# A one-layer streaming encoder: where cross attention's operands, some sums, the first weight and the last stores stand

## The chip, the cores and the metric

The kernel runs on one core of a Trainium2 chip. The metric is the time of one execution on the device in microseconds; the time before is a median of three runs. The engines are named as in the profile: PE multiplies matrices and PEld loads its stationary operand, DVE, ACT and POOL work on vectors, SP issues most of the transfers between DRAM and the core's memory. An engine runs its instructions in the order in which they stand in its row; between engines, semaphores make one wait for another.

## The reference

One layer is applied to 1024 prompt frames and 32 sample frames, which share the weights. Cut to what matters:

```python
h = rms_norm(x, g_mix)
q, k, v, ch, cb, cc, ga, gb = split(h @ w_in)
a = window_attention(q, k, v) @ w_attn_out
bo = (cb * causal_conv3(cc * ch)) @ w_conv_out
x = x + (sigmoid(ga) * a + sigmoid(gb) * bo) @ w_mix_out
cq = rms_norm(x, g_cross) @ w_cq              # 4 heads of 64
p = softmax(cq @ mem_k.T * 64 ** -0.5)        # 256 memory tokens
x = x + (p @ mem_v) @ w_co
x = x + relu(rms_norm(x, g_mlp) @ w_up) ** 2 @ w_down
y = rms_norm(x, g_final)
```

The width is 1024 and the hidden width of the MLP 4096, all in FP32. The memory's keys and values are computed from the prompt's memory tokens, and given as a cache for the sample.

## The kernel before

**Products.** An FP32 operand is split in a rounded high part and the rest, and a product is made of three matmuls: high by high, high by low and low by high (`gemm`, lines 195 to 197, and `product`, 866 to 868). The 1056 frames are treated as three chunks, `CH`, of 384, 384 and 288 columns, with the features on the partitions. A feature block of an output takes eight groups of three matmuls.

**Weights.** A block of 128 output features is a tile of 128 x 1024, 512 KB. `fetch_w` (L155) lets SP load it to `wr`; `issue_w` has ACT cast the high part `wh` (L129) and DVE subtract the low part `wl` (L130). Two raw tiles take turns, with a third at times, and two weights are made ready ahead (`LOOK`). For weights that come again with the next chunk, the dict `kept` holds low parts: at the first use `wl` is stored to DRAM (L174), later it is loaded (L168) and only the cast is done (L169).

**Start.** `norm_x` loads the first chunk's x (`raw`, L302) in four pieces, the parameters `prm` (L304) and the first weights, all on SP. ACT and DVE make the high and low parts of each feature of x (`X`, L274 and L275): two features, then the first weight, then six.

**Middle.** Per chunk, `trunk` gives eight products conv_out (`do_conv_out`: evacuation L1051, addition L1052, split to `M`) and eight products mix (`do_mix`: L1066, with x loaded by L1062). Cross attention takes its keys from `mem_key` (loads L1077) and its values from `mem_val` (load L1086, cast L1089, subtraction L1090); `mem_load` and `mem_load_s` do all of one kind at a place of the program. Scores are L1141, exponents L1146, output products L1204 to L1206 with the evacuation L1208. The first products of the MLP run beside the third chunk's trunk and cross attention: their evacuations are L1325 to L1356. `sums_early(k)` makes sums of normalised x for a later step of the MLP (L1380 to L1383, split by L1374 and L1375), `late_tiles` and `sums_first` the sums of the last columns.

**End.** `final_last` scales six tiles of 128 x 512 by the last norm (L1829 on DVE, L1831 on ACT), and SP stores them (L1833).

**Order.** The program is written as items: products are fillers, and between them come the calls that `then(i, ...)` and the third argument of `beside` put behind filler i. A scheduler that simulates the engines moves instructions among each other where data allow it; what stands in `pin` keeps the order of the program, and in a `manual_schedule` region the named engines keep the order written. So a call's place is a wish for most instructions and binding for pinned ones.

Of the kernel before, what the change touches and what calls it, by code (L numbers as in the profile page):

```python
# [10 lines left out]
F32 = mybir.dt.float32  # L11
# [7 lines left out]
P = 128  # L19
# [4 lines left out]
NF = 8  # L24
# [16 lines left out]
def hybrid_step(ctx: ExitStack, tc: tile.TileContext, io):  # L41
    nc = tc.nc
    act, dve, pool_e, pe, sp = nc.scalar, nc.vector, nc.gpsimd, nc.tensor, nc.sync
# [3 lines left out]
    def nm(s):  # L47
        uid[0] += 1
        return f"{s}_{uid[0]}"
# [12 lines left out]
    wp = ctx.enter_context(tc.tile_pool(name="wp", bufs=3))  # L62
# [31 lines left out]
    mk_d = dram.tile([2, P, 256], F32, name="mk_d")  # L94
    mv_d = dram.tile([2, P, 256], F32, name="mv_d")

    def pin(ins):
        return tc.keep_in_program_order(ins)
# [29 lines left out]
    def split(hi, lo, src):  # L128
        act.copy(hi, src)  # L129
        dve.tensor_sub(lo, src, hi.bitcast(F32))  # L130
# [26 lines left out]
            pin(load)  # L157
        fetched.append(raw)

    def issue_w():  # L160
        if not fetched:
            fetch_w()
        raw = fetched.pop(0)
        key = worder[wpos[0]]
        hi = wp.tile([P, 1024], F32R, tag="wh", name=nm("wh"))
        lo = wp.tile([P, 1024], F32R, tag="wl", name=nm("wl"))
        if kept.get(key) is not None:
            sp.dma_start(lo.bitcast(F32), kept[key])  # L168
            act.copy(hi, raw)  # L169
        else:  # L170
            split(hi, lo, raw)
            if key in kept:
                kept[key] = dram.tile([P, 1024], F32, name=nm("wl_d"))
                sp.dma_start(kept[key], lo.bitcast(F32))  # L174
        ready.append((worder[wpos[0]], (hi, lo)))
        wpos[0] += 1
# [101 lines left out]
    W = {}  # L278
# [11 lines left out]
    def norm_x():  # L290
        pool_e.memset(ones, 1.0)
        act.copy(ones_r, ones.to_broadcast([P, P]))
        warm = misc.tile([P, 1], F32, name="warm")
        act.activation(warm, ones, AF.Sqrt)
        make_identity(nc, ident)
        raws = []

        def load_x():
            for c, (o, n) in enumerate(CH):
                raw = raw_tile()[:, : NF * n].rearrange("p (f t) -> p f t", f=NF)  # L300
                for h in range(4):
                    sp.dma_start(raw[:, 2 * h : 2 * h + 2], io[f"x{c}"][:, 2 * h : 2 * h + 2])  # L302
                    if c == h == 0:
                        sp.dma_start(prm, io["params"])  # L304
                        fetch_w()
                if c == 0:
                    fetch_w()
                    fetch_w()
                raws.append(raw)

        def parts(c, fs, pinned=lambda x: x):
            for f in fs:
                xg[c][f] = (slot(xpool, f"X{c}", CH[c][1]), slot(xpool, f"X{c}", CH[c][1]))
                scaled_split(*xg[c][f], raws[c][:, f], G_MIX + f, pinned)

        def squares(c):
            n = CH[c][1]
            acc = st.tile([P, n], F32, tag="sum", bufs=2, name=nm("sum"))
            for f in range(NF):
                sq = st.tile([P, n], F32, tag="sq", bufs=2, name=nm("sq")) if f else acc  # L320
                (pin if c else lambda x: x)(act.activation(sq, raws[c][:, f], AF.Square))
                if f:
                    dve.tensor_add(acc, acc, sq)
            accs[c] = [acc]

        with tc.manual_schedule(engines={mybir.EngineType.SP}):
            load_x()
        with tc.manual_schedule(engines={mybir.EngineType.Activation, mybir.EngineType.DVE}):
            parts(0, range(2))
            issue_w()  # L330
            parts(0, range(2, NF))
            issue_w()
            issue_w()
            squares(0)
        wk, wv = ready[0][1], (ready[1][1], ready[2][1])
        kt = at_tile([P, NT], F32, "kt")
        ktt[0] = kt
        vs3 = {}

        def scaled(c):  # L340
# [731 lines left out]

    def mem_key(src, tag, bufs=1):

        t = cr.tile([P, 256], F32, tag="mkr", bufs=1, name=nm("mkr"))
        for e in range(2):
            sp.dma_start(t[64 * e : 64 * e + 64], src)  # L1077
        hi = cr.tile([P, 256], F32R, tag=f"{tag}h", bufs=bufs, name=nm("mkh"))
        lo = cr.tile([P, 256], F32R, tag=f"{tag}l", bufs=bufs, name=nm("mkl"))
        split(hi, lo, t)  # L1080
        return hi, lo

    def mem_val(src, tag):

        t = cr.tile([P, 256], F32, tag="mkr", bufs=1, name=nm("mvr"))
        sp.dma_start(t, src)  # L1086
        v = cr.tile([P, 4, 2, 64], F32R, tag=tag, name=nm("mv"))
        s3 = t.rearrange("p (h d) -> p h d", h=4)
        act.copy(v[:, :, 0], s3)  # L1089
        dve.tensor_sub(v[:, :, 1], s3, v[:, :, 0].bitcast(F32))  # L1090
        return v

    pkeys, pvals, svals = [], [], []

    def mem_load():
        pkeys.extend(mem_key(mk_d[h // 2, 64 * (h % 2) : 64 * (h % 2) + 64], "pk", 4) for h in range(4))
        pvals.extend(mem_val(mv_d[j], f"pv{j}") for j in range(2))

    def mem_load_s():
        svals.extend(mem_val(io["cmem_v"][j], f"sv{j}") for j in range(2))  # L1100

    qc, co = {}, [[None, None] for _ in CH]

# [509 lines left out]

    def cross_steps(c):

        steps = [("call", [mem_load if c == 0 else mem_load_s])]
        steps.append(("call", [lambda: chunk_stats(c)]))
        steps.append(("items", [(do_cq(c, j), ("w_cq", j)) for j in range(2)]))
        for i, step in enumerate(cross_units(c)):
            steps.append(step)  # L1620
            if i < 4 - c:
                steps.append(("call", []))
        if c:
            steps.append(("call", []))
# [23 lines left out]
        ]  # L1648

    for name, n in (("w_conv_out", NF), ("w_mix", NF), ("w_cq", 2), ("w_co", 2)):  # L1650
        kept.update(((name, j), None) for j in range(1, n, 2) if (name, j) != ("w_conv_out", 5))

    trunks = [trunk(c) for c in range(3)]
    trunks[0].insert(NF, trunks[1].pop(0))
    left = beside(
        [], trunks[0], [(i, lambda: pump(2)) for i in range(NF)] + [(12, lambda: third.update(n=0, pool=W["pool"]))]
    )
    item(lambda: pump(0))
    left = beside(cross_steps(0), trunks[1])
# [14 lines left out]
    def then(i, *what):  # L1674
        at.setdefault(i, []).extend(what)

    call = lambda fn, *args: lambda: item(lambda: fn(*args))
    assert len(left) == 1
    then(0, *[call(x) for x in left[0][1]], call(mem_load_s))
    then(1, call(chunk_stats, 1))  # L1680
    then(2, *[lambda j=j: item(do_cq(1, j), ("w_cq", j)) for j in range(2)])
    for f in range(NF):
# [19 lines left out]
    then(34, lambda: item(do_co(2, 0), ("w_co", 0)))  # L1702
    then(35, lambda: item(do_co(2, 1), ("w_co", 1)))
    for k in range(4):
        then(34 + k, call(sums_early, k))
    then(36, call(open_late), call(chunk_col, 2))
    then(37, call(chunk_row, 2))
    then(38, call(late_tiles))
# [96 lines left out]
    def final_last(c):  # L1805
# [19 lines left out]
        for i, (j, h) in enumerate([(0, 1), (1, 1), (2, 1), (0, 0), (1, 0), (2, 0)]):  # L1825
            tag, bufs = homes[i]
            y = wp.tile([P, 512], F32, tag=tag, bufs=bufs, name=nm("y"))
            if i % 2:
                dve.tensor_scalar_mul(y, turned[j][:, h], RC[c][:, j : j + 1])  # L1829
            else:  # L1830
                act.mul(y, turned[j][:, h], RC[c][:, j : j + 1])  # L1831
            rows = slice(96, P) if j == 2 else slice(0, P)
            sp.dma_start(io[f"y{c}"][j, rows, 512 * h : 512 * h + 512], y[rows])  # L1833

    A11, A21, A12, A22 = (0, 0), (0, 4), (1, 0), (1, 4)
    steps = [(j, t) for j in range(4) for t in range(2)]
# [151 lines left out]
```

## Time and profile before

| what | value |
|---|---|
| median of 3 runs (lowest to highest) | 1761.08 us (1759.91 to 1767.39) |
| the profiled execution | 1762.53 us, span 1760.8 |
| granted PE clock, mean | 0.996 |
| DMA over the span | mean 198 GB/s, 348.18 MB |

Times in rows are microseconds from the span's start. A row of the timeline gives the start, the duration, engine, line, operation, the output and inputs by the program's names, and in brackets how long the engine stood idle before it and what it waited for. Rows marked x2 or x6 are several alike. The rows of the stretches give for each engine busy time and, in brackets, the number of instructions; then the granted clock, the share of the DMA engines and the rate. SP's rows are the requests, not the transfers themselves.

### The profile page before, as it was taken

Reading aid. Unit: us, or ns where it says so; the run is one execution under the profiler, and the core shown is the slowest. Engines: PE = TensorE matmul, PEld = TensorE weight load, DVE = VectorE, ACT = ScalarE, POOL = GpSimd, SP = SyncE. Lnnn points to the kernel's source line nnn. Section 1 sums busy time; section 2 is a strip of 40 time slices with the busy share of each in tenths; the row PEclk is TensorE's granted clock in tenths of the full one; section 3 lists DMA queues with packets and bytes.
Section 4 is the critical chain, followed back from the end, with each engine's and each line's share of the span. In section 5 each row is a group of like instructions: output and inputs, shape, how many; then the busy total and the mean of one; then the engine's idle time right before and its main releaser. Section 6 shows DMA issues by size and latency. Waiting matters only on the chain.

```text
span 1760.8 us, 32586 instructions
## 1 busy us (share of the span) xinstructions
PE 1726.3 (98%) x12250; PEld 1710.8 (97%) x12250; DVE 1189.4 (68%) x2272; ACT 853.7 (48%) x1660; POOL 585.0 (33%) x667
## 2 busy tenths in 40 slices
PE   8999999999999999999899999999999999999998
PEld 8999999999999999999899999999999999999998
DVE  6776776768666647546567777787666686546675
ACT  8653534535335325335456665774444464333443
POOL 0026366453552545441225132005555410000121
PEclk9999999999999999999999999999999999999999
DMA  5243334333436888867755667675666786554554
GB/s 184 95 131 124 118 132 152 118 135 127 157 142 206 292 288 298 265 218 251 265 200 198 233 215 237 217 245 195 221 221 222 229 313 201 183 195 161 198 169 159
DMA packets 179997, 348.18 MB, mean 198 GB/s; under 512 B 18672, under 2 KB 100880, under 8 KB 179712
## 3 DMA queue, kind: packets, MB, share of 16 engines
q1 hardware_dynamic: 164272, 292.42, 49.6%
q0 software_dynamic: 15568, 53.68, 8.6%
q8 instruction: 96, 1.57, 0.4%
q14 instruction: 61, 0.50, 0.1%
HBM read 251.77 MB, written 93.67 MB: 196 GB/s over the span
## 4 chain that ended last, share of the span: by engine, by line
PE 52%; DMA 4%; DVE 2%; ACT 2%; POOL 1%; issue 1%; DVEq 0%; SPq 0%; POOLq 0%; ACTq 0%
PE acc L1773 6%; PE acc L1774 6%; PE acc L1775 6%; PE acc L866 5%; PE acc L867 5%; PE acc L868 5%; PE acc L195 3%; PE acc L197 2%; PE acc L196 2%; PE pc L867 2%; PE pc L868 2%; PE pc L866 2%; DMA ct<-m_d 1%; DMA ct<-in_x 1%; PE pa L196 1%
## 5 line engine op out<-in xcount | busy, mean ns | idle before, releaser
L129 ACT CAST wh<-wr 128x1024 fp32r<-128x1024 f32 x228 | 239.4, 1050 | 419.6 <-PE acc L1774 128.6
L130 DVE TENSOR_TENSOR wl<-wr,wh 128x1024 fp32r<-128x1024 f32 x228 | 295.6, 1296 | 130.9 <-ACT wh L129 129.3
L195 PE MATMUL acc<-X,wh 128*128 128x384 f32 (+1 forms) x864 | 282.1, 326 | 8.0 <-ACT wh L129 8.0
L196 PE MATMUL acc<-X,wh 128*128 128x384 f32 (+1 forms) x864 | 279.2, 323 | 0.0
L197 PE MATMUL acc<-X,wl 128*128 128x384 f32 (+1 forms) x864 | 278.6, 322 | 0.2 <-DVE wl L130 0.2
L271 POOL TENSOR_TENSOR xacc<-xacc,ct 128x384 f32<-128x384 f32 (+1 forms) x56 | 75.5, 1351 | 382.2 <-ACT ct L269 380.6
L195 PEld LDWEIGHTS acc<-X,wh 128*128 128x128 f32 x864 | 163.1, 189 | 8.6 <-ACT wh L129 8.0
L196 PEld LDWEIGHTS acc<-X,wh 128*128 128x128 f32 x864 | 163.4, 189 | 0.6
L197 PEld LDWEIGHTS acc<-X,wl 128*128 128x128 f32 x864 | 163.0, 189 | 0.8 <-DVE wl L130 0.8
L195 PE MATMUL acc<-Y,wh 128*128 128x384 f32 (+1 forms) x432 | 140.4, 327 | 4.1 <-DVE ct L1051 3.3
L197 PE MATMUL acc<-Y,wl 128*128 128x384 f32 (+1 forms) x432 | 140.5, 326 | 2.4 <-DMA wl<-wl_d 2.4
L196 PE MATMUL acc<-Y,wh 128*128 128x384 f32 (+1 forms) x432 | 140.5, 326 | 0.0
L1774 PE MATMUL acc<-n,wh 128*128 128x264 f32 x352 | 100.2, 285 | 0.0
L1773 PE MATMUL acc<-n,wh 128*128 128x264 f32 x352 | 100.2, 285 | 0.0
L1775 PE MATMUL acc<-n,wl 128*128 128x264 f32 x352 | 99.9, 284 | 0.0
L129 ACT CAST PTh<-pt 128x512 fp32r<-128x512 f32 (+3 forms) x94 | 45.8, 517 | 110.8 <-PE pt L584 109.7
L721 POOL TENSOR_TENSOR ws<-ws 128x256 f32<-128x256 f32 x100 | 93.1, 931 | 5.8 <-DMA ws<-in_w_up 0.2
L721 POOL TENSOR_TENSOR xacc<-xacc 128x256 f32<-128x256 f32 x100 | 87.6, 876 | 5.7 <-DMA xacc<-in_w_in 0.3
L195 PEld LDWEIGHTS acc<-Y,wh 128*128 128x128 f32 x432 | 82.0, 190 | 5.3 <-DVE ct L1051 4.2
L197 PEld LDWEIGHTS acc<-Y,wl 128*128 128x128 f32 x432 | 82.3, 191 | 2.8 <-DMA wl<-wl_d 2.8
L196 PEld LDWEIGHTS acc<-Y,wh 128*128 128x128 f32 x432 | 82.1, 190 | 0.3 <-DVE Y L777 0.3
L570 ACT ACTIVATE S<-S,nmx 128x257 f32<-128x257 f32 (+1 forms) x132 | 64.2, 488 | 20.7 <-DVE nmx L565 19.4
(424 smaller groups left out, 5503.1 us busy)
## 6 DMA issues: line engine op xcount, KB each, us to landing
wr<-in_w_in SPq DMA_DIRECT2D x53, 512.0 KB, 3.6
wr<-in_w_up SPq DMA_DIRECT2D x53, 512.0 KB, 4.7
wr<-wsum_d SPq DMA_DIRECT2D x40, 512.0 KB, 3.4
wr<-in_w_conv_out SPq DMA_DIRECT2D x24, 512.0 KB, 4.5
wr<-in_w_mix SPq DMA_DIRECT2D x24, 512.0 KB, 5.0
wr<-in_w_down SPq DMA_DIRECT2D x24, 512.0 KB, 3.5
n_d<-Z SPq DMA_DIRECT2D x32, 264.0 KB, 4.4
xacc<-in_w_down POOLq DMA_DIRECT2D x16, 512.0 KB, 4.2
```

The source lines that it names most:

```text
L129: act.copy(hi, src)
L130: dve.tensor_sub(lo, src, hi.bitcast(F32))
L195: pe.matmul(out, wh[:, a], hi, start=(k == 0), stop=False)
L196: pe.matmul(out, wh[:, a], lo, start=False, stop=False)
L197: pe.matmul(out, wl[:, a], hi, start=False, stop=(k == len(acts) - 1))
L721: pin(pool_e.tensor_tensor(t[:, to], t[:, x], t[:, y], op=ALU.add))
L866: pe.matmul(acc, wh[:, a], hi, start=(start and k == 0), stop=False, skip_group_check=True)
L867: pe.matmul(acc, wh[:, a], lo, start=False, stop=False, skip_group_check=True)
L868: pe.matmul(acc, wl[:, a], hi, start=False, stop=(k == 3), skip_group_check=True)
L1773: pe.matmul(a, wh[:, s], hi, start=(t == 0 and k == 0), stop=False, skip_group_check=True)
L1774: pe.matmul(a, wh[:, s], lo, start=False, stop=False, skip_group_check=True)
L1775: pe.matmul(a, wl[:, s], hi, start=False, stop=(t == 1 and k == 7), skip_group_check=True)
```

## The change

1. **First weight.** Its request stands in ACT's row, ahead of everything there, and no more in SP's. One feature of x is split before it in place of two, and the weight is split in two pieces, 256 and 768 columns.
2. **Operands of cross attention.** Four keys and two values of the memory and two values of the sample are loaded one per mix product of the first chunk. Their splits are pinned, and their raw tiles have two buffers in place of one.
3. **Kept low parts.** The conv_out weight 3 is no more among them: each chunk splits it again.
4. **Early sums.** `sums_early(k)` stands behind filler 35 + k in place of 34 + k.
5. **Last stores.** Those of tiles that ACT scales are requested by ACT.

The core of the diff:

```diff
-    def issue_w():
+    def issue_w(pieces=(slice(0, 1024),)):
...
-            split(hi, lo, raw)
+            for at in pieces:
+                split(hi[:, at], lo[:, at], raw[:, at])
...
                         sp.dma_start(prm, io["params"])
-                        fetch_w()
...
+        first_raw = wp.tile([P, 1024], F32, tag="wr", bufs=2, name=nm("wr"))
+        with tc.manual_schedule(engines={mybir.EngineType.Activation}):
+            act.dma_start(first_raw, weight(worder[0]))
+        fetched.append(first_raw)
...
-            parts(0, range(2))
-            issue_w()
-            parts(0, range(2, NF))
+            parts(0, range(1))
+            issue_w((slice(0, 256), slice(256, 1024)))
+            parts(0, range(1, NF))
...
-        t = cr.tile([P, 256], F32, tag="mkr", bufs=1, name=nm("mkr"))
+        t = cr.tile([P, 256], F32, tag="mkr", bufs=2, name=nm("mkr"))
...
-        split(hi, lo, t)
+        if bufs == 4:
+            pin(act.copy(hi, t))
+            pin(dve.tensor_sub(lo, t, hi.bitcast(F32)))
+        else:
+            split(hi, lo, t)
...
-        act.copy(v[:, :, 0], s3)
-        dve.tensor_sub(v[:, :, 1], s3, v[:, :, 0].bitcast(F32))
+        pin(act.copy(v[:, :, 0], s3))
+        pin(dve.tensor_sub(v[:, :, 1], s3, v[:, :, 0].bitcast(F32)))
...
-        steps = [("call", [mem_load if c == 0 else mem_load_s])]
+        steps = [("call", [])]
...
-        [], trunks[0], [(i, lambda: pump(2)) for i in range(NF)] + [(12, lambda: third.update(n=0, pool=W["pool"]))]
+        [], trunks[0], [(i, lambda: pump(2)) for i in range(NF)]
+        + [(12, lambda: third.update(n=0, pool=W["pool"]))] + [(NF + 1 + i, fn) for i, fn in enumerate(mem_loads)]
...
-    then(0, *[call(x) for x in left[0][1]], call(mem_load_s))
+    then(0, *[call(x) for x in left[0][1]])
...
-        then(34 + k, call(sums_early, k))
+        then(35 + k, call(sums_early, k))
...
-            sp.dma_start(io[f"y{c}"][j, rows, 512 * h : 512 * h + 512], y[rows])
+            (sp if i % 2 else act).dma_start(io[f"y{c}"][j, rows, 512 * h : 512 * h + 512], y[rows])
```

Beside these, `mem_loads` is a list of the eight loads, each a call of `mem_key` or `mem_val`, and `("w_conv_out", 3)` joins the exception in the loop that fills `kept`. The lines of the changed kernel are shifted: L1051, L1066, L1086, L1090, L1208, L1380 and L1833 become L1055, L1070, L1094, L1098, L1215, L1387 and L1841.

ACT's row at the start, before, where `wr` is the loaded first weight and `X` the parts of x:

```order
L292 ACT_TABLE_LOAD
L292 CAST ones_r<-ones 128x128
L294 ACT_TABLE_LOAD
L294 ACTIVATE warm<-ones 128x1
L274 ACTIVATE X_7_165<-raw_140,prm 128x384
L274 ACTIVATE X_9_169<-raw_140,prm 128x384
L129 CAST wh_173<-wr_143 128x1024
L274 ACTIVATE X_13_177<-raw_140,prm 128x384
```

and now:

```order
L328 DMA wr_138<-in_w_in 128x1024
L293 ACT_TABLE_LOAD
L293 CAST ones_r<-ones 128x128
L295 ACT_TABLE_LOAD
L295 ACTIVATE warm<-ones 128x1
L275 ACTIVATE X_7_168<-raw_145,prm 128x384
L129 CAST wh_172<-wr_138 128x256
L129 CAST wh_172<-wr_138 128x768
L275 ACTIVATE X_11_178<-raw_145,prm 128x384
```

The request leads the row, and one `X` stands ahead of the weight's two casts.

DVE's row at the last conv_out products of the first chunk and the first mix products, before. The first number of a name is the buffer or copy; `mv` are values, `wl` weights, `M` and `Y` activations:

```order
L797 TENSOR_TENSOR Y_1654_9618<-ct_9569,Y_1653_9617 128x288
L1090 TENSOR_TENSOR mv_10177<-mvr_10175,mv_10177 128x4x64
L130 TENSOR_TENSOR wl_9728<-wr_9725,wh_9727 128x1024
L130 TENSOR_TENSOR M_9662<-ct_9658,M_9661 128x384
L797 TENSOR_TENSOR Y_1666_9666<-ct_9621,Y_1665_9665 128x288
L797 TENSOR_TENSOR Y_1668_9670<-ct_9623,Y_1667_9669 128x288
L1090 TENSOR_TENSOR mv_10182<-mvr_10180,mv_10182 128x4x64
L1051 TENSOR_TENSOR ct_9710<-acc_9685,Gb_1562_9252 128x384
L1051 TENSOR_TENSOR ct_9760<-acc_9735,Ga_1110_6654 128x384
L1052 TENSOR_TENSOR ct_9710<-ct_9710,ct_9683 128x384
L130 TENSOR_TENSOR wl_9770<-wr_9767,wh_9769 128x1024
L130 TENSOR_TENSOR M_9714<-ct_9710,M_9713 128x384
```

and now from the addition of the first chunk's eighth conv_out product (L1052 before, L1056 now) on; `mkl` are keys:

```order
L1056 TENSOR_TENSOR ct_9713<-ct_9713,ct_9686 128x384
L130 TENSOR_TENSOR wl_9731<-wr_9728,wh_9730 128x1024
L130 TENSOR_TENSOR M_9717<-ct_9713,M_9716 128x384
L801 TENSOR_TENSOR Y_1679_9721<-ct_9676,Y_1678_9720 128x288
L801 TENSOR_TENSOR Y_1681_9725<-ct_9678,Y_1680_9724 128x288
L1055 TENSOR_TENSOR ct_9763<-acc_9738,Ga_1110_6659 128x384
L130 TENSOR_TENSOR wl_9773<-wr_9770,wh_9772 128x1024
L130 TENSOR_TENSOR M_9767<-ct_9763,M_9766 128x384
L1070 TENSOR_TENSOR Ga_1696_9803<-acc_9778,ct_9776 128x384
L130 TENSOR_TENSOR wl_9820<-wr_9817,wh_9819 128x1024
L276 SCALAR_TENSOR_TENSOR Y_1698_9806<-Ga_1696_9803,prm,Y_1697_9805 128x384
L1086 TENSOR_TENSOR mkl_9814<-mkr_9810,mkh_9813 128x256
```

The value that stood ahead of L1051 is gone from there; the first key follows the first mix product's evacuation (L1070) and low part.

DVE's row at the end of the third chunk's cross attention, before, where `Ga` and `Gb` are the evacuated output products and `ct` the sums:

```order
L1208 TENSOR_TENSOR Ga_2186_11851<-acc_13550,Ga_2186_11851 128x288
L1208 TENSOR_TENSOR Ga_2216_11977<-acc_13561,Ga_2216_11977 128x288
L1208 TENSOR_TENSOR Gb_2233_12045<-acc_13572,Gb_2233_12045 128x288
L1380 TENSOR_TENSOR ct_13583<-n_2546_13460,n_2554_13468 128x240
L1208 TENSOR_TENSOR Gb_2252_12138<-acc_13634,Gb_2252_12138 128x288
L1381 TENSOR_TENSOR ct_13584<-t_2538_13452,ct_13583 128x240
L1382 TENSOR_TENSOR ct_13585<-t_2538_13452,n_2546_13460 128x240
L130 TENSOR_TENSOR wl_13631<-wr_13628,wh_13630 128x1024
L1208 TENSOR_TENSOR Gb_2271_12228<-acc_13645,Gb_2271_12228 128x288
L1383 TENSOR_TENSOR ct_13586<-n_2562_13476,ct_13584 128x240
L1208 TENSOR_TENSOR Gb_2304_12380<-acc_13655,Gb_2304_12380 128x288
```

and now:

```order
L1215 TENSOR_TENSOR Ga_2215_11980<-acc_13564,Ga_2215_11980 128x288
L1215 TENSOR_TENSOR Gb_2232_12048<-acc_13575,Gb_2232_12048 128x288
L1215 TENSOR_TENSOR Gb_2251_12141<-acc_13621,Gb_2251_12141 128x288
L130 TENSOR_TENSOR wl_13618<-wr_13615,wh_13617 128x1024
L1215 TENSOR_TENSOR Gb_2270_12231<-acc_13632,Gb_2270_12231 128x288
L1215 TENSOR_TENSOR Gb_2303_12383<-acc_13642,Gb_2303_12383 128x288
L1215 TENSOR_TENSOR Gb_2316_12438<-acc_13652,Gb_2316_12438 128x288
L1387 TENSOR_TENSOR ct_13662<-n_2545_13463,n_2553_13471 128x240
L1388 TENSOR_TENSOR ct_13663<-t_2537_13455,ct_13662 128x240
L1389 TENSOR_TENSOR ct_13664<-t_2537_13455,n_2545_13463 128x240
L130 TENSOR_TENSOR wl_13681<-wr_13678,wh_13680 128x1024
```

Three of the evacuations stood behind the first sums; now all stand ahead of them.

More of the change, by code (lines that the diff above doesn't have):

```diff
@@ L1079, in mem_key @@
         lo = cr.tile([P, 256], F32R, tag=f"{tag}l", bufs=bufs, name=nm("mkl"))
-        split(hi, lo, t)
+        if bufs == 4:
[3 more added lines that the diff above has]
+            split(hi, lo, t)
         return hi, lo
     def mem_val(src, tag):
-        t = cr.tile([P, 256], F32, tag="mkr", bufs=1, name=nm("mvr"))
+        t = cr.tile([P, 256], F32, tag="mkr", bufs=2, name=nm("mvr"))
         sp.dma_start(t, src)
@@ L1088, in mem_val @@
         s3 = t.rearrange("p (h d) -> p h d", h=4)
-        act.copy(v[:, :, 0], s3)
-        dve.tensor_sub(v[:, :, 1], s3, v[:, :, 0].bitcast(F32))
+        pin(act.copy(v[:, :, 0], s3))
+        pin(dve.tensor_sub(v[:, :, 1], s3, v[:, :, 0].bitcast(F32)))
         return v
     pkeys, pvals, svals = [], [], []
[L1095 to L1100, printed above, removed]
+    mem_loads = [
+        lambda h=h: pkeys.append(mem_key(mk_d[h // 2, 64 * (h % 2) : 64 * (h % 2) + 64], "pk", 4)) for h in range(4)
+    ]
+    mem_loads += [lambda j=j: pvals.append(mem_val(mv_d[j], f"pv{j}")) for j in range(2)]
+    mem_loads += [lambda j=j: svals.append(mem_val(io["cmem_v"][j], f"sv{j}")) for j in range(2)]
     qc, co = {}, [[None, None] for _ in CH]
@@ L1650, in hybrid_step @@
     for name, n in (("w_conv_out", NF), ("w_mix", NF), ("w_cq", 2), ("w_co", 2)):
-        kept.update(((name, j), None) for j in range(1, n, 2) if (name, j) != ("w_conv_out", 5))
+        kept.update(((name, j), None) for j in range(1, n, 2) if (name, j) not in (("w_conv_out", 3), ("w_conv_out", 5)))
     trunks = [trunk(c) for c in range(3)]
```

## The prediction

> **What bounds the kernel now.** I read the page's busy times first, then PE's waits, then the timeline around each of them. PE's row says that the kernel is PE time with small holes.
>
> ```profile
> PE 1726.3 (98%) x12250; PEld 1710.8 (97%) x12250; DVE 1189.4 (68%) x2272; ACT 853.7 (48%) x1660; POOL 585.0 (33%) x667
> PE acc L195 <- ACT wh L129: 8.0, 1, 8.0
> PE acc L195 <- DVE ct L1051: 5.0, 4, 1.9
> PE acc L866 <- ACT lt L1355: 2.8, 2, 1.7
> PE sc L1141 <- ACT S L1146: 1.1, 1, 1.1
> ```
>
> PE is idle 1760.8 − 1726.3 = 34.5 us of the span: 8.0 before the first matmul, about 7.5 after the last (tail rows below), and some 19 in holes of at most 2.5. The change adds and removes no matmul of the products, so it can gain only from these 34.5 us. The columns of the last four rows are: us in total, times, longest; two more waits, of 2.45 and 1.90, stand below with their places.
>
> **The start.** Four rows set the end of the first hole; the others show what follows.
>
> ```profile
> 0.74 0.40 SPq L302 DMA_DIRECT2D raw<-in_x  x1
> 1.20 0.41 SPq L304 DMA_DIRECT2D prm<-in_params  x1
> 1.66 0.42 SPq L155 DMA_DIRECT2D wr<-in_w_in  x1
> 4.34 1.12 ACT L274 ACTIVATE X<-raw,prm 128x384 fp32r<-128x384 f32 x2 [0.52 <-DMA prm<-in_params]
> 6.92 1.04 ACT L129 CAST wh<-wr 128x1024 fp32r<-128x1024 f32 x1 [1.45 <-DMA wr<-in_w_in]
> 7.99 1.22 DVE L130 TENSOR_TENSOR wl<-wr,wh 128x1024 fp32r<-128x1024 f32 x1 [1.86 <-ACT wh L129]
> 8.01 0.69 PE L195 MATMUL acc<-X,wh 128*128 128x384 f32 x1 [8.01 <-ACT wh L129]
> 9.13 3.26 DVE L275 SCALAR_TENSOR_TENSOR X<-raw,prm,X 128x384 fp32r<-128x384 f32 x6
> 10.72 0.52 PE L195 MATMUL acc<-X,wh 128*128 128x384 f32 x1
> 11.04 0.52 PE L196 MATMUL acc<-X,wh 128*128 128x384 f32 x1
> 13.32 0.34 PE L195 MATMUL acc<-X,wh 128*128 128x384 f32 x1
> 13.50 0.33 PE L196 MATMUL acc<-X,wh 128*128 128x384 f32 x1
> ```
>
> The weight, asked for at 1.66, is what ACT waits for (1.45 us), and PE waits for the cast. The change moves that request to ACT's first row, at about 0.73 (SP's first is at 0.74), 0.93 earlier. If all of it reaches the landing, the weight is there at 5.99. The casts' price comes from two lengths: 1024 columns take 1.04 and 384 take 1.12/2 = 0.56, so about 0.27 + 0.75 per 1000 columns: 0.46 for the piece of 256 and 0.85 for 768. DVE's two pieces are about 0.45 and 0.96 by the same way (1.22; 3.26/6 = 0.54). The first matmul starts at 5.99 + 0.46 = 6.45. But the second feature's high part now stands behind both casts and its low part behind both subtractions: casts to 7.30, X high to 7.86, subtractions to 8.33, X low to 8.87. PE waits there, ends the second feature's group of three matmuls at 0.32 each by 9.5, and starts the third at 9.5; before it was 10.72. That is 1.2 early.
>
> The other end: raw, prm and the weight now share the transfer engines. If the weight lands only when before all three had, at 6.92, only the pieces are gained: the third group starts at 10.47, 0.25 early. PE's pace changes within these rows, from 0.32 (10.72 to 11.04) to 0.18 (13.32 to 13.50). If the change of pace stays at its hour, work moved ahead of it is worth half: 0.13 to 0.6; if it comes earlier with the start, up to 2.0. A loss is possible if prm is held back too: landed with the others at 6.92, it lets X of feature 0 end at 7.5, the first cast at 7.9, the second at 8.8, the second feature's X at 9.4 and its low part, behind both subtractions, at about 10.4; the third group then starts at 11.0, 0.3 late. SP's own later requests come 0.42 earlier, without the weight's row among them, which nothing here waits for. I take −0.7, the middle of early and late landing with most of the pace; the ends are −2.0 and +0.3.
>
> [...]
>
> **Cross attention's operands.** Eight loads and their splits were scattered; four of the values stand here.
>
> ```profile
> 837.05 0.32 SPq L1086 DMA_DIRECT2D mvr<-mv_d  x1
> 840.78 0.41 ACT L1089 CAST mv<-mvr 128x256 fp32r<-128x256 f32 x1 [2.83 <-DMA mvr<-mv_d]
> 841.22 0.43 DVE L1090 TENSOR_TENSOR mv<-mvr,mv 128x256 fp32r<-128x256 f32 x1 [1.86 <-ACT mv L1089]
> 842.17 0.45 PE L195 MATMUL acc<-M,wh 128*128 128x384 f32 x1 [1.64 <-DVE ct L1051]
> 849.46 0.41 ACT L1089 CAST mv<-mvr 128x256 fp32r<-128x256 f32 x1 [2.66 <-DMA mvr<-in_cmem_v]
> 850.35 1.14 SPq L1077 DMA_DIRECT2D mkr<-in_cmem_k  x2
> 852.13 0.44 PE L197 MATMUL acc<-M,wl 128*128 128x384 f32 x1 [0.50 <-DVE wl L130]
> 866.83 1.23 DVE L130 TENSOR_TENSOR wl<-wr,wh 128x1024 fp32r<-128x1024 f32 x1
> 868.98 0.89 SPq L168 DMA_DIRECT2D wl<-wl_d  x1
> 876.12 0.44 PE L197 MATMUL acc<-Y,wl 128*128 128x384 f32 x1 [2.45 <-DMA wl<-wl_d]
> 842.00:878.00 36.00, 32.71 (x180) 31.75 (x181) 21.59 (x32) 16.98 (x30) 7.57 (x6) 0.98 0.75 259
> ```
>
> At 837.05 SP asks for a value; ACT stands 2.83 us for it and DVE 1.86, and the evacuation L1051 behind them lets PE wait 1.64. The same at 849.46 delays a weight: 0.50. The order now has nothing of memory ahead of the last conv_out evacuations, so I take both as gone: 2.14. The new splits, 0.41 on ACT and 0.43 on DVE in each of eight mix products, fit: DVE works 21.59 of 36 us there, and eight splits add 3.4 to that at most.
>
> The 2.45 is the end of a late stream: the low part, asked for at 868.98 behind its weight's split of 866.83, lands at 876.1, 7.1 later. With PE 2.14 ahead, it must land by 871.5. SP's rows of operands, such as the 1.14 at 850.35 ahead of the next weight, are now asked for by the place of their split, and I let the stream come one mix product earlier: 24 matmuls at 0.17 to 0.18, or 4.2 us. A landing at 871.9 leaves 0.4. So 2.0 of 2.45 gained, and −4.1 together. The ends: 0, if the operands wait as before, and −4.6 (2.14 + 2.45).
>
> **One kept low part less.** It takes away a store and two reloads of 512 KB and adds two subtractions of 1.22. In the third chunk it falls into this stretch:
>
> ```profile
> 975.40:979.70 4.30, 4.30 (x30) 4.30 (x30) 0.16 (x2) 1.49 (x3) 0.00 (x0) 1.00 1.02 374
> ```
>
> DVE works 0.16 of 4.30 us while PE is never idle: the subtraction costs nothing, and 1.2 if that cover is gone. I leave it at 0.
>
> **Sums one place later.** Before, the first of them stand between the evacuations of the last cross output product.
>
> ```profile
> 1138.50 0.98 DVE L1380 TENSOR_TENSOR ct<-n,n 128x240 f32<-128x240 f32 x1
> 1139.78 0.39 DVE L1381 TENSOR_TENSOR ct<-t,ct 128x240 f32<-128x240 f32 x1
> 1140.09 1.01 DVE L1382 TENSOR_TENSOR ct<-t,n 128x240 f32<-128x240 f32 x1
> 1141.02 1.82 DVE L130 TENSOR_TENSOR wl<-wr,wh 128x1024 fp32r<-128x1024 f32 x1
> 1142.77 0.44 DVE L1208 TENSOR_TENSOR Gb<-acc,Gb 128x288 f32<-128x288 f32 x1
> 1143.26 0.39 PE L866 MATMUL acc<-Y,wh 128*128 128x264 f32 x1 [1.90 <-DVE Gb L1208]
> 1150.40 0.41 DVE L1383 TENSOR_TENSOR ct<-n,ct 128x240 f32<-128x240 f32 x1 [2.42 <-PE pq L226]
> 1161.68 1.23 DVE L130 TENSOR_TENSOR wl<-wr,wh 128x1024 fp32r<-128x1024 f32 x1 [1.08 <-ACT wh L129]
> ```
>
> All eight L1208 now stand ahead of the first sum, so the 1.90 goes. About 2.4 us of DVE's work (0.98 + 0.39 + 1.01) moves behind them; the 2.42 and 1.08 of idle time later take it. The last key of the sample, fetched earlier now, puts its scores ahead, and I count half of the 1.1 us at L1141. The 2.8 at L1355 is ACT's crowd of copies and stays. Sum −2.5. The ends: −4.7 (1.9 + 1.1 + 1.7), if the longer L1355 wait and the rest of L1141's go too, and +3, if the fourth group of sums meets the late ones.
>
> **The tail.**
>
> ```profile
> 1754.21 1.84 ACT L1831 ACTIVATE y<-acc,rc 128x512 f32<-128x512 f32 x3 [0.89 <-DVE rc L233]
> 1754.23 2.12 DVE L1829 TENSOR_SCALAR y<-acc,rc 128x512 f32<-128x512 f32 x3
> 1754.93 2.77 SPq L1833 DMA_DIRECT2D out_y<-y  x6
> ```
>
> Six requests take 2.77 on SP, 0.46 each, to 1757.70; the span ends 3.1 later. With three on ACT, in its row behind the scalings: 1.84 + 3 × 0.46 from 1754.21 ends at 1757.43. SP's three end by 1756.8. So −0.3; the ends are 0, as the bytes are the same, and −0.8, if the last bytes follow SP's end.
>
> **The sum.** −0.7 − 4.1 + 0 − 2.5 − 0.3 = −7.6 us. The profiled execution took 1762.53 (span 1760.8), 1.4 over the median of the runs, so its own forecast is 1754.9; the median's is 1761.08 − 7.6 = 1753.5. About 0.5%, or 8.8 us, is what a measurement here can tell from no change; my forecast lies just inside.
>
> **The rivals.**
> 1. The stream stays late. The transfers in 842 to 878 already move 259 GB/s, and the operands bring the same bytes into the same products; then the reload's 2.45 stays and grows by the 2.14 that PE gains ahead of it. For it speaks the 7.1 us landing, against it that 374 GB/s were moved at 975. Mix term near 0: 1757.6.
> 2. The wait moves (the slower side). The buffers of the operands are two; the third to eighth load waits on SP for DVE's split two products back, with the loads of the evacuations' inputs behind it, and ACT's and DVE's rows hold their splits in order. If each of these six stands as the one at 841.22 did, PE pays 6 × 1.64 = 9.8. Mix term −4.1 + 9.8: 1763.3. It decides from five such waits on (8.2 against 7.6). The split is due two products (8.3 us) after the load is asked for, and a landing took 3.7 (837.05 to 840.78), so it needs landings beyond about 7, as the reload's.
> 3. Sums collide. The fourth group now falls on the step that makes the late tiles, eight instructions of 0.41 (one is the row at 1150.40), 3.3 us of DVE work in a stretch whose idle time is the 1.08; if PE waits 3 for weights there, beside the gain of 2.5 kept: 1756.5, and 1759.0 if that gain is lost too.
> 4. Nothing changes at the start, since the weight lands at 6.92 and pace does the rest: 1754.2; it is inside the first case.
>
> **Chances.** The forecast with its start variants 0.55, of which 0.36 end below 1752.3, where the start's clock and the sums' other waits give more; its own range is 1749 to 1757. Late stream 0.17, all within 0.5%. Moved waits 0.14, of which 0.08 beyond +0.5% if they draw the sums along. Collision 0.14, 0.04 of it slower, 0.02 faster. Faster 0.38, same 0.50, slower 0.12. The range 1749 to 1763 takes the best ends of the sum nearly whole (−2.0 − 4.6 − 4.7 − 0.8 = −12.1) and reaches rival 2.
>
> **What would show it.** Right: first matmul near 6.5 to 7.4 with a wait on X low after it; no PE wait on L1055 near 840; no DMA wait on a reload near 871; L1215 eight times before the first L1387; last store requests on two engines by 1757.5. Wrong: ACT or DVE idle on mkr or mvr in the mix products, evacuations that follow PE by more than one product, PE waits on wl between 1160 and 1190. The number fails if the reload's hole only shifts, or if holes open elsewhere in the tens of microseconds that follow, where the order of DVE and ACT has moved by a few rows.

## The result

The changed kernel takes 1756.07 us in the median of 20 runs (1751.64 to 1759.89), the kernel before 1761.17 (1758.28 to 1768.44). The ratio is 0.9966, 95% interval 0.9955 to 0.9976: about 6 us less by the ratio, between 4 and 8; the medians differ by 5.1. The forecast was 7.6 less. The runs of one kernel lie up to 10 us apart, so one profile is no measure of a few microseconds, and this was the trap of the case: its first profile, of an execution of 1754.54 with a span of 1752.8, shows 8 less than the profile before.

The page and PE's waits after, as those shown before (line, what it waited for, us in total, times, longest):

```profile
PE 1724.4 (98%) x12250; PEld 1710.3 (98%) x12250; DVE 1190.7 (68%) x2275; ACT 853.7 (49%) x1661; POOL 583.9 (33%) x667
PE acc L196 <- ACT wh L129: 7.0, 1, 7.0
PE acc L196 <- DVE ct L1055: 3.4, 3, 1.9
PE acc L870 <- ACT lt L1362: 2.2, 1, 2.2
PE pr L244 <- ACT ct L242: 1.7, 1, 1.7
```

The waits on the reloaded low part, on L1208 (now L1215) and on the scores are not there. A wait of 1.7 us on the statistics of the first chunk is new: `pr` is the row broadcast of the normalisation. Some 185 us ahead of that, a wait of 1.0 on a weight's low part is gone, one of 1.2 on a weight's cast is new, and one on `Ga` (L988, before L984) grew from 0.4 to 1.5. At the start:

```profile
0.73 0.41 ACTq L328 DMA_DIRECT2D wr<-in_w_in  x1
1.20 0.44 SPq L305 DMA_DIRECT2D prm<-in_params  x1
6.08 0.61 ACT L275 ACTIVATE X<-raw,prm 128x384 fp32r<-128x384 f32 x1 [1.82 <-DMA prm<-in_params]
6.61 1.12 ACT L129 CAST wh<-wr 128x256 fp32r<-128x256 f32 x2
7.05 0.69 PE L196 MATMUL acc<-X,wh 128*128 128x384 f32 x1 [7.05 <-ACT wh L129]
9.30 0.69 PE L197 MATMUL acc<-X,wh 128*128 128x384 f32 x1 [0.32 <-DVE X L276]
10.11 0.52 PE L196 MATMUL acc<-X,wh 128*128 128x384 f32 x1
13.95 0.52 PE L196 MATMUL acc<-X,wh 128*128 128x384 f32 x1
15.27 0.28 PE L206 MATMUL acc<-wh,X 128*128 128x256 f32 x1
```

The parameters landed at 6.0, before at 4.3; ACT waited for them and no more for the weight. The third group begins at 10.11 in place of 10.72. But the matmuls were still at the slow pace at 13.95 (0.32 apart to 14.27, 0.17 to 0.18 from 14.57 on), and the next product begins at 15.27, before at 14.89. At the reload, at the sums and in the tail:

```profile
865.49 0.45 SPq L168 DMA_DIRECT2D wl<-wl_d  x1
889.83 0.45 PE L244 MATMUL pr<-ct,ones_r 128*128 128x384 f32 x1 [1.72 <-ACT ct L242]
1134.03 1.34 DVE L1215 TENSOR_TENSOR Gb<-acc,Gb 128x288 f32<-128x288 f32 x3
1135.28 0.65 DVE L1387 TENSOR_TENSOR ct<-n,n 128x240 f32<-128x240 f32 x1
1176.56 0.39 PE L870 MATMUL acc<-t,wh 128*128 128x264 f32 x1 [2.20 <-ACT lt L1362]
1745.20 0.16 DVE L234 SCALAR_TENSOR_TENSOR rc<-st_t,st_y 128x3 f32<-128x3 f32 x1
1746.25 1.71 SPq L1841 DMA_DIRECT2D out_y<-y  x3
1746.76 1.15 ACTq L1841 DMA_DIRECT2D out_y<-y  x2
```

The last requests end 2.76 after `rc`, before 3.74 (1757.70 less 1753.96). Yet the span ends 7.60 after it, before 6.84.

### The profile page after: what moved, and what is told of

Its sections match the earlier page's. It is cut to its first block, busy times and chain, and to the rows that moved or that the text cites. A ratio compares the mean times of both kernels' runs of the same rounds, so it can differ in the third digit from the quotient of the medians.

```text
span 1752.8 us, 32573 instructions
## 1 busy us (share of the span) xinstructions
PE 1724.4 (98%) x12250; PEld 1710.3 (98%) x12250; DVE 1190.7 (68%) x2275; ACT 853.7 (49%) x1661; POOL 583.9 (33%) x667
## 4 chain that ended last, share of the span: by engine, by line
PE 53%; DMA 3%; DVE 2%; ACT 1%; POOL 1%; issue 1%; SPq 0%; DVEq 0%; POOLq 0%; ACTq 0%
PE acc L1781 6%; PE acc L1782 6%; PE acc L1783 6%; PE acc L870 6%; PE acc L871 6%; PE acc L872 6%; PE acc L196 2%; PE acc L198 2%; PE acc L197 2%; PE pc L871 2%; PE pc L872 2%; PE pc L870 2%; DMA ct<-in_x 1%; DMA ct<-m_d 1%; POOL ct L1056 1%
## 5 line engine op out<-in xcount | busy, mean ns | idle before, releaser
L129 ACT CAST wh<-wr 128x1024 fp32r<-128x1024 f32 (+1 forms) x231 | 241.6, 1046 | 411.8 <-PE acc L1782 132.2
L130 DVE TENSOR_TENSOR wl<-wr,wh 128x1024 fp32r<-128x1024 f32 (+1 forms) x231 | 295.6, 1280 | 129.5 <-ACT wh L129 127.7
L725 POOL TENSOR_TENSOR ws<-ws 128x256 f32<-128x256 f32 x100 | 87.1, 871 | 5.6
```

The costliest lines, as they stand in the source:

```text
L725: pin(pool_e.tensor_tensor(t[:, to], t[:, x], t[:, y], op=ALU.add))
```

## The experiments

My theory after the result: each part's holes had the prices read from the profile. The rivals: the start and the stores give nothing or lose, and the reload's hole is a matter of chance, so that the first profile after was a lucky one. The parts were run alone and together, each beside the kernel before. "Kept part" means that the low part of conv_out 3 is kept no more. A ratio under 1 is faster.

| what differs from the kernel before | ratio | 95% interval |
|---|---|---|
| operands alone | 0.9987 | 0.9974 to 0.9999 |
| sums alone | 0.9990 | 0.9979 to 1.0002 |
| start alone | 0.9995 | 0.9982 to 1.0009 |
| stores alone | 1.0008 | 0.9998 to 1.0019 |
| operands and kept part | 0.9984 | 0.9974 to 0.9994 |
| kept part alone | 0.9991 | 0.9980 to 1.0003 |
| operands, kept part, sums | 0.9979 | 0.9970 to 0.9989 |
| the same, statistics early | 0.9976 | 0.9965 to 0.9987 |
| all of the change, again | 0.9976 | 0.9964 to 0.9989 |
| operands, sums, two kept parts dropped | 0.9993 | 0.9978 to 1.0007 |
| the same, statistics early | 0.9978 | 0.9963 to 0.9994 |
| the same, a third form of the start | 1.0010 | 0.9998 to 1.0023 |

### Operands alone

The edit takes `mem_key`, `mem_val`, `mem_loads` and their places from the change, with two buffers and pins, and nothing else:

```diff
+        + [(NF + 1 + i, fn) for i, fn in enumerate(mem_loads)]
```

> The operands' part alone, the rest as before. Theory (the gain is there): PE has no wait on the evacuation near 840 and none on a reloaded low part near 874; the granted clock from 874 to 882 stays above 0.95 where the profile of before has 0.79; the holes of before there, 4.8 us, and about 1.3 us of slowed matmuls go, a hole of about 1.7 us opens at the prompt's statistics of the first chunk behind it; 4 to 5 us faster in all. Rival (a late stream, the wait moves): the reload's hole stays above 1.5 us or new holes open in the mix products; within 2 us of before.

0.9987, some 2.3 us (0.2 to 4.6), between theory and rival. PE's waits from 835 to 895:

```profile
PE pr L243 <- ACT ct L241: 3.1, 1, 3.1
PE acc L197 <- DMA wl<-wl_d: 1.6, 1, 1.6
PE acc L195 <- ACT M L129: 1.0, 1, 1.0
```

The evacuation's wait is gone, but one on `M` of 1.0 stands near it. The reload still holds PE, and what it won ahead of that, the statistics take with 3.1. One gain lies elsewhere: from 1090 to 1190 the waits on the scores (1.1) are gone and those on the last evacuations of cross attention fall from 1.9 to 0.6, though the sums stand as before.

### Sums alone

```diff
-        then(34 + k, call(sums_early, k))
+        then(35 + k, call(sums_early, k))
```

> The early sums one place later, alone. Theory: the wait on the evacuation of the cross output products (1.9 us) goes and nothing takes its place; the wait at the sample's scores (1.1 us) stays, since the operands are as before; 1.5 to 2.5 us faster. Rival (collision with the late sums): the waits between 1150 and 1190 grow by as much; within 1 us of before.

0.9990, some 1.8 us. The wait on L1208 is gone, as expected; four of the eight evacuations had stood behind the first sum in the profile before (at 1139.41, 1142.77 and two at 1143.68), not three. From 1090 to 1190 PE's waits fall from 6.0 to 2.1. The collision did not come between 1150 and 1190, but a little later; PE's waits from 1186 to 1208 in this run:

```profile
PE pc L867 <- DVE b L1298: 1.0, 2, 0.7
PE acc L866 <- DVE Z L1503: 0.8, 1, 0.8
PE pc L866 <- DVE Z L1524: 0.6, 1, 0.6
```

These 2.4 us are in the profile of one other run, the last one, and in none of the rest: in two of the eight profiles that have this edit, and in none of the six without it. So not every execution pays them; whether the edit makes them possible is not shown.

### Start alone

```diff
+            act.dma_start(first_raw, weight(worder[0]))
...
+            parts(0, range(1))
+            issue_w((slice(0, 256), slice(256, 1024)))
+            parts(0, range(1, NF))
```

> The first weight on ACT's queue with one feature and two pieces, alone. Theory (shared transfers): the parameters land near 6.0 in place of 4.3, the first matmul starts near 7.0, the third group of matmuls 0.5 to 0.7 us early; the first values product starts between 0.6 us early and 0.4 us late, by the hour at which the pace doubles; time 0 to 0.6 us faster. Rival (as its profile showed it, a loss by 50 us of about 0.5): the pace doubles late again, by over 1 us after 12.96; 0.3 to 0.6 us slower.

0.9995: nothing that can be told. The first matmul at 6.99, the third group at 10.05, the product of the values at 15.33. Over three profiles with this start (this, the changed kernel, and the changed kernel again) that product begins at 15.33, 15.27 and 14.56; over ten with the old start at 14.17 to 15.63, their mean 15.0. The lead of 0.6 at the third group is spent by the pace.

### Stores alone

```diff
-            sp.dma_start(io[f"y{c}"][j, rows, 512 * h : 512 * h + 512], y[rows])
+            (sp if i % 2 else act).dma_start(io[f"y{c}"][j, rows, 512 * h : 512 * h + 512], y[rows])
```

> The last six stores on two queues, alone. Theory (requests were the limit): from the last reciprocal to the end of the span 0.3 to 1.0 us less than the 6.8 of before. Rival (the landing is the limit): the last request ends about 1 us earlier, and the end comes at the same distance from the reciprocal, 6.8 us, or later by up to 0.8 as in the changed kernel.

1.0008, as the rival had it; the time alone does not tell it from no change (0.9998 to 1.0019), the profiles do. From `rc` to the end it is 7.42 us; with the changed kernel 7.60 and in its second profile 7.49. The eleven profiles with one queue have 6.61 to 7.01. Transfers of the last stores: first the kernel before (a 256 KB store lands in 2.4), then the second profile of the changed kernel:

```profile
out_y<-y SPq DMA_DIRECT2D x4, 256.0 KB, 2.4
```

```profile
out_y<-y ACTq DMA_DIRECT2D x2, 256.0 KB, 3.4
out_y<-y SPq DMA_DIRECT2D x2, 256.0 KB, 3.2
```

Requests end a microsecond sooner, and each large store takes 0.8 to 1.0 longer there: the edit loses about 0.7, by the means of the three and of the eleven. So issue time was saved here (the last request ends 2.8 after `rc`, before 3.7), and more than that was lost at the landing.

### Operands with the kept part, and the kept part alone

```diff
-        kept.update(((name, j), None) for j in range(1, n, 2) if (name, j) != ("w_conv_out", 5))
+        kept.update(((name, j), None) for j in range(1, n, 2) if (name, j) not in (("w_conv_out", 3), ("w_conv_out", 5)))
```

> The operands' part with the kept low part of conv_out 3 dropped, the rest as before. Theory (the dropped store and reload free SP's row and the transfers in the mix products): the reload of the second chunk's first kept weight is asked for before 867 and PE does not wait for it, where the operands alone left 1.55 us; no wait at the evacuation near 840; 3.5 to 5 us faster than before. Rival (the kept part is worth nothing, and the operands' gain is chance of one execution): the reload's hole of 1 to 2.5 us stays; 1 to 2.5 us faster, as the operands alone.

> The kept low part of conv_out 3 dropped, alone. Theory (it frees transfers, but the operands still stand in the way): the hole at the reload shrinks to 1 to 2 us; 0.5 to 2 us faster. Rival (nothing, as I had put it): within 0.5 us of before, the holes at 840, 850 and 874 of the size they have in the runs with those parts unchanged, 0.4 to 1.6, 0.3 to 0.7 and 1.5 to 2.5 us.

0.9984 and 0.9991: beside the operands' 0.9987, the kept part is worth nothing that can be told, and alone at most some 3.5 us. The reload's wait of the first, from 835 to 895, is that run's only one:

```profile
PE acc L197 <- DMA wl<-wl_d: 2.4, 1, 2.4
```

So the operands and kept part do clear the mix products of the other waits, but not of this one. The kept part alone has 1.7 there. So neither the rival, that it is worth nothing, nor a gain of its own is excluded.

### The change without start and stores, and the statistics earlier

The first has operands, kept part and sums. The second adds

```diff
-        steps = [("call", [])]
-        steps.append(("call", [lambda: chunk_stats(c)]))
+        steps = [("call", [lambda: chunk_col(c)])]
+        steps.append(("call", [lambda: chunk_row(c)]))
```

> The changed kernel with start and stores as before, so operands, kept part and sums. Theory (start and stores give nothing or lose): 6 to 7 us faster than before, no less than the changed kernel's 6. Rival (the start gives 0.7 and the stores 0.3): 5 us faster, less than the changed kernel.

> As the run with operands, kept part and sums, and the first chunk's sum of squares and reciprocal asked for one product earlier, with the row broadcast where it was. Theory (a new wait has taken the place of those removed: the statistics stand behind a split on DVE): the wait of 1.7 us on the broadcast's operand near 888 goes, and it is 1 to 2 us faster than that run. Rival (the earlier sum of squares waits for POOL instead): a wait on POOL of 1 us or more near 881 and no gain.

0.9979 and 0.9976: neither is told from the changed kernel, nor from each other. Both have the reload's wait, 2.2 and 2.6, and neither one on the statistics. So the theory of a new wait in the place of the old could not show itself here: in these two PE waits at the reload, and the statistics are in time. That is no rule, as the run with the operands alone had both, 1.6 and 3.1.

### The changed kernel again

No edit.

> The changed kernel once more, with a profile of its own. Theory (its first profile fell on an execution in which the reload came in time; the four others with the operands' part had a hole of 1.6 to 2.6 us there): the hole at the reload near 872 is 1 to 2.6 us again, slowed matmuls may follow it, and the hole at the statistics near 888 is gone or small; the time is again 5 to 6 us under before. Rival (start and operands together remove it): no wait on the reload, 1.7 us at the statistics as in the first profile. For the end both expect 5.8 to 6.0 us from the last scale factor's row to the end of the span, against 5.2 to 5.4 with one queue.

0.9976, and in its profile the reload is back:

```profile
PE acc L198 <- DMA wl<-wl_d: 2.3, 1, 2.3
```

It was asked for at 866.37, 0.88 later than in the first profile, and PE had its matmuls ready from 871.14; the low part was there 7.1 after the request. In the first profile PE used it without a wait at 871.70, 6.2 after the request. The program is the same, so the hole's absence in the first profile lay in the execution, not in the edit. All profiles of kernels with this reload, with the granted clock of PE from 870 to 890:

| profile | hole at the reload | clock 870 to 890 |
|---|---|---|
| before | 2.45 | 0.91 |
| sums alone | 1.45 | 1.00 |
| start alone | 1.91 | 0.91 |
| stores alone | 2.21 | 0.91 |
| kept part alone | 1.71 | 1.00 |
| operands alone | 1.55 | 1.00 |
| operands and kept part | 2.40 | 0.91 |
| without start and stores | 2.21 | 0.91 |
| the same, statistics early | 2.62 | 0.83 |
| changed, first | none | 1.00 |
| changed, again | 2.29 | 0.91 |

Five profiles without the operands' part have 1.45 to 2.45, mean 1.9; six with it have 0 to 2.62, mean 1.8.

### Without the reload

A second low part, that of conv_out 1, is kept no more; then the same with the statistics early.

```diff
-        kept.update(((name, j), None) for j in range(1, n, 2) if (name, j) != ("w_conv_out", 5))
+        kept.update(((name, j), None) for j in range(1, n, 2) if name != "w_conv_out" or j == 7)
```

> As the run with operands, kept part and sums, and conv_out 1 dropped from the kept as well, so that each chunk splits it: the reload at which PE waits is not there. Theory (the reload is a hole of 2 us and what comes behind it is hidden by it): no wait near 872; a wait of 1 to 3 us at the statistics near 888 to 891 takes most of it; 0.5 to 1 us faster than the run with the reload. Rival (the raw weight comes as late as the reload did): a wait of 1 to 2.5 us on ACT's or DVE's split near 872, no gain.

> The same with the first chunk's statistics asked for one product earlier. Theory: neither the wait at the reload nor the one at the statistics; 1.5 to 3 us faster than with the reload, 6 to 7.5 us faster than before. Rival (a third wait follows, on POOL's sum of squares or on an evacuation): holes of 1 us or more between 876 and 900; 4 to 5 us faster than before.

0.9993 and 0.9978. PE's waits from 835 to 895, the first run's, then the second's:

```profile
PE pr L243 <- ACT ct L241: 1.6, 1, 1.6
```

```profile
PE pr L244 <- DVE ct L242: 0.6, 1, 0.6
PE pq L226 <- POOL xacc L271: 0.5, 1, 0.5
```

The chain is shown: with the reload gone, PE waits for the statistics, and with these earlier, 1.1 us of smaller waits are left. Between the mix products and the statistics (861 to 880) the first gains 4.3 us on the kernel before, the hole's 2.45 and its slowed matmuls. It does not keep them. From 960 to 1010, where the kernel before waits for three evacuations, this run's waits are

```profile
PE acc L195 <- DVE ct L1051: 3.0, 2, 1.5
PE o L1180 <- ACT PTh L129: 1.4, 1, 1.4
PE o L1180 <- DVE PTl L130: 0.7, 1, 0.7
```

The two on `PT`, the turned scores, 2.1 in all, are new. The weight that is split in place of being reloaded gives ACT and DVE work in the third chunk, and it stands beside the second chunk's cross attention. That this split is what delays `PT` was not tried. The second run has the two waits on `PT` as well, and behind them PE ran at half pace for nearly 7 us, 3.4 us lost; the last three numbers are the clock, the share of the transfers and GB/s:

```profile
1000.00:1012.00 12.00, 9.19 (x43) 7.91 (x43) 10.26 (x24) 8.09 (x24) 3.30 (x4) 0.72 0.65 214
```

That takes a good part of what it had won ahead, and it is no faster than the runs with the reload.

### A third form of the start

On top of that, the parameters are asked for ahead of x, and two features are split ahead of the weight's pieces.

```diff
+                    if c == h == 0:
+                        sp.dma_start(prm, io["params"])
                     sp.dma_start(raw[:, 2 * h : 2 * h + 2], io[f"x{c}"][:, 2 * h : 2 * h + 2])
...
+            parts(0, range(2))
```

> The same, and at the start the first weight on ACT's queue, the parameters ahead of x on SP's, two features split ahead of the weight, and the weight in two pieces. Theory (the changed start lost its lead since the parameters landed at 6.0 and low parts of x stood behind the weight's): X starts before 5.3, the first matmul at 6.0 to 6.8, no wait behind it, the third group by 9.4; 1 us faster than the run without it, less 0.5 if the pace doubles at its hour. Rival (the transfers share, all land near 6.5): the first matmul after 7, no gain.

1.0010, some 5 us over the run without it. Its start is not at fault by its profile: the first matmul at 7.60 had no wait behind it, the third group began at 9.77 and the values at 14.44, the earliest but one of all. X waited now for x itself, 1.88 us, until 6.13, with the parameters there by 4.95: x landed near the rival's 6.5 and the first matmul came after 7, but the parameters did not land with them. The loss lies later: 2.4 on an evacuation of the queries where the run before had 0.9, and the same 2.4 between 1186 and 1208 as in the run with the sums alone. From 14 to 1740 PE idles 15.7 us, against 12.3 in the run before it. Why a start should bring these out stays open. None of the twelve beats the changed kernel.

## Why the prediction was right, and where its terms were not

The time lies in the range and the sign is right; 7.6 forecast, 4 to 8 measured, 6 likeliest, and 4.2 in the second comparison. The range, 1749 to 1763, holds the kernel before as well, so lying in it shows little, and the total comes nearer than its terms do, in part by luck: start, operands and tail gave less than forecast, the waits of the sums more. The mechanism, holes of PE that close, is borne out: from 14 to 1740 PE idles 18.7 us before (1726.00 less 1707.32 busy), and 12.8 and 12.9 in the two profiles of the changed kernel. But the step that the change "can gain only from these 34.5 us" of idle time failed: a matmul at half pace counts as busy (from 874 to 882 the run with operands and kept part has PE busy for all of the 8.00 us, at a granted clock of 0.86), and the profile before loses some 5 us to such stretches, as shown in the last section. The terms:

- **Start, −0.7.** Failed. The two bounds were right for the landing: it fell between them, the parameters came late, and the third group was 0.6 early. What I gave to the pace, "the middle of early and late landing with most of the pace", was wrong: in three profiles the product of the values starts on average where it did. 0 is the size.
- **Operands, −4.1.** This is the term that was mis-sized most. I read the holes of one execution as the kernel's. The 1.64 at the evacuation was the largest of five profiles with the old operands (1.64, 1.20, 0.35, 0.38, and 0.6 on another operand); the mean is 0.8. The 0.50 at the weight has a mean of 0.4. Both do go when the operands and the kept part are moved. The step "I let the stream come one mix product earlier" failed: SP asked 2.6 us sooner in the second profile of the changed kernel (868.98 to 866.37), and PE came there 2.5 us sooner (873.67 to 871.14), so the hole stayed. This was rival 1, which I gave 0.17. The time of the part alone is −2.3, and part of that is at 1106 and 1143, where I had put nothing on its account beside half of the scores' wait.
- **Kept part, 0.** Not told from 0, with the operands (0.9984 beside 0.9987) or alone.
- **Sums, −2.5.** Right as to the 1.90, which is in no profile with this edit. From 1090 to 1190 the kernel before waits 6.0 us. With the operands alone it is 3.6, with operands, kept part and sums 2.2, and in the two profiles of the changed kernel 2.2 and 3.0. So 3 to 3.8 go, more than the term says. The two parts' gains overlap: the operands alone take 2.4 of them, and the sums alone 3.9. The operands end the whole wait at the scores, of which I counted half (it is 0 to 1.15 in the five profiles with the old operands and in none with the new), and most of that on L1208. With the whole change, of the waits on ACT's copies, which I left as they were, the shorter, 1.05, is gone or down to 0.4, and the longer grew from 1.73 to 2.20.
- **Tail, −0.3.** Wrong in sign. Requests end 2.7 to 2.8 after `rc`, sooner than the 3.5 that I put (1757.43 less 1753.96), and the landing takes that and 0.7 more. My bound of 0 from below had "as the bytes are the same" as its reason, and that reason does not exclude a loss.

Rival 2, waits that move to the third to eighth operand, did not come: in no profile does PE wait for a split of an operand, and the mix products of the changed kernel have no hole ahead of the reload. Rival 4 has the size that the start had, but not its reason: the first cast began at 6.61, so the weight had landed before the 6.92 of that rival, and what held the cast was the parameters. Rival 3 did not come where I put it; waits on DVE's rows are seen after 1186 in two profiles, one of them with the sums alone, and what makes them was not found.

## What to carry to other kernels

A hole that hangs on when a transfer lands differs from one execution to the next: here 0 and 2.29 in two executions of one program, and 0.35 to 1.64 at another place in four kernels whose edits lie elsewhere. Before a term is priced by such a hole, look at two or three profiles of the kernel, and price it by their mean; and ask not only whether the late transfer is asked for sooner, but whether the engine that needs it comes sooner by as much. Each of the seven holes of 1.9 us or more at the reload had 1.7 us or more behind it in slowed matmuls, so that removing such a hole can be worth nearly double, and the next wait may lie just under it: 1.6 us at the statistics here, with the reload gone. Before two profiles are compared, add up their slowed matmuls over the whole span: in two executions of the changed kernel they come to 4.2 and 10.2 us, and differ by as much as the change is worth.

## What the runs showed of the hardware

**A hole of about 2 us at the reload was followed by half pace of PE.** Stretches from 874 to 882, first of the kernel before, with its hole at 876, then of the changed kernel's first profile without one (after the engines' busy times the granted clock, the share of the transfers and GB/s):

```profile
874.00:882.00 8.00, 5.88 (x25) 5.88 (x26) 2.98 (x4) 2.57 (x5) 1.49 (x2) 0.79 0.85 296
```

```profile
874.00:882.00 8.00, 8.00 (x50) 8.00 (x49) 7.08 (x9) 3.75 (x7) 3.82 (x3) 1.00 0.61 189
```

In the first, matmuls begin 0.32 apart from 876.58 to 879.78, and 0.17 apart from 880.04. A clock lower by 0.21 over 8 us is 1.7 us lost, or 3.4 us at half pace. In the table above each of the seven holes of 1.9 or more is followed by such a loss, twice as much after the 2.62, and none of the three of 1.45 to 1.71.

That is no threshold, as other places show. The wait on an evacuation near 1000, of 1.86 to 1.88, came with a clock of 0.86 from 1000 to 1012 in two profiles, before and changed again, and 1.00 in the others with that size. A hole of 1.54 at 978 was followed by half pace in the first run without the reload, and holes of 1.54 there in the two runs after it were not. Two short holes a microsecond apart near 1002 were followed by twice the usual loss in the second run without the reload (1.42 and 0.67) and in the run after it (0.97 and 0.67), and by none in the first (1.36 and 0.67). And the changed kernel's first profile has such a stretch near 1142, with no hole of PE in the 7 us ahead of it; what stands there are 24 matmuls of one column, from 1137.97 to 1140.57:

```profile
1140.00:1150.00 10.00, 10.00 (x72) 10.00 (x72) 9.01 (x27) 7.60 (x20) 0.00 (x0) 0.83 0.75 290
```

Every profile has two to six such stretches between 14 and 1740, of 1.7 us lost or twice that. Counted from the granted clock in steps of 2 us, they cost 5.1 us before, 4.2 in the first profile of the changed kernel (0.7 of it at the very end), and 10.2 in its second. As PE's idle time is the same in those two, these stretches are nearly all of the 5.8 us by which their spans differ, 1752.8 and 1758.6. What starts a stretch without a hole, those matmuls or something else, stays open.

At the start PE ran at half pace too, with matmuls 0.32 apart, and then rose to 0.17 to 0.18 apart. With the changed start it rose 7.5 us (7.05 to 14.57), 7.8 and 6.6 us after the first matmul, in three profiles that all have a wait of 0.3 on X low at 9.0 to 9.3, and 4.3 to 6.8 after it with the old start. What sets that hour was not shown.

**Two issuers made stores slower.** The same 1.18 MB at the end took 7.50 us on average from `rc` to the end of the span with ACT and SP as issuers, in place of 6.83, and the three profiles of the one kind lie above all eleven of the other, as shown with the stores alone. Why was not tried.
